# Output projection and second MLP product in seven quarter products instead of eight

## Chip, cores and metric

One core of a Trainium2 chip runs the kernel. The metric is the device time in microseconds. The five engines keep their own instruction queues and run them in order: TensorE (PE, with its weight loads PEld), VectorE (DVE), ScalarE (ACT), GpSimd (POOL) and SyncE (SP), which here only issues DMAs. TensorE writes its sums into PSUM; weights and activations lie in SBUF, and all inputs come from HBM by DMA.

## What is computed

One layer of a hybrid decoder block on 512 tokens of width 1024. Four token mixers are merged under gates (`mixed`), then an output projection, a residual, a second RMSNorm and an MLP follow:

```python
    proj = jnp.einsum('bsnc,ncd->bsnd', ys, w_branch[l])
    gates = jax.nn.sigmoid(jnp.einsum('bsd,de->bse', xn, w_gate[l]) + b_gate[l]).reshape(B, S, N_MIXERS, D)
    mixed = jnp.sum(gates * proj, axis=2)
    x = x + jnp.einsum('bsd,de->bse', mixed, w_out[l])
    hn = _rms(x, norm2_g[l])
    hid = jnp.square(jax.nn.relu(jnp.einsum('bsd,df->bsf', hn, w_mlp1[l])))
    x = x + jnp.einsum('bsf,fd->bsd', hid, w_mlp2[l])
```

`w_out` is 1024 x 1024, `w_mlp1` 1024 x 4096, `w_mlp2` 4096 x 1024, all float32.

## The kernel before

**Products in three matmuls.** Every float32 operand is split into a rounded part and a rest (`split`, L73 to L76): ScalarE casts the source to the type `F32R` (`hi`, L74), VectorE subtracts it from the source (`lo`, L75). `mm3` (L78 to L81) then issues three matmuls, hi x hi, hi x lo and lo x hi, into one PSUM sum. A matmul takes a 128 x 128 stationary operand and streams up to 512 columns.

**Weight stream.** `pieces` is the list of weight pieces in the order of use. `piece` (L91) gives each a `load`, a DMA on SyncE's queue (L102) into one of four `raw` buffers of 128 x 1024 floats, and a `make`, which splits the raw piece into `hi` and `lo`, three buffers each. `take` (L123) returns the next piece, makes two pieces ahead of it and loads two further.

**Order of the work.** The Tile planner (L1065) puts each engine's instructions in order when the kernel is built, from simulated times, the earlier in the program first among those ready. On the chip an engine then runs its list in that order and waits by semaphores.

**Stages.** Projections, attention, gating and convolutions come first; the last of them is `gate_branch` (from L797), where each of eight 128-column blocks `dt` of `MIX` (features on partitions, tokens along the free side) gets its last term, and in the last branch VectorE's sum is at once split into `MH`, `ML`. GpSimd adds the terms of the middle branches (L828). Then:
- *Output projection* (L923 to L944): for each half `q` of the output columns and each of four token tiles `t`, eight k-tiles times three matmuls of 512 columns, 192 in all. L936 adds the sum to the residual `X1`; ScalarE squares it, and for `q == 1` `norm_scale` (L300) and `norm_tr` (L309, eight transposes) make the normed, transposed, split input `HH`, `HL` of the MLP. `tr_task` puts the transposes of one tile between later matmuls.
- *MLP* (L967 to L1019): for each half `fh` of the 32 blocks of hidden features, first the product with `w_mlp1` (24 matmuls of 512 columns a block, `mlp1_part`; relu on ScalarE, square on VectorE L961, split into `hdh`, `hdl`); the very first three blocks run their first 256 tokens before the second 256, which gives the last norms time (L971 to L978). Then `out_mm` (L996) for each half `q` of the output columns: eight pieces of two hidden blocks each, 24 matmuls a piece, 768 over the four passes; L1017 adds to `X1`, and the last passes store the output. The last tile is cut into two halves of 256 columns.

Of the kernel before, what the change touches and what calls it, by code (L numbers as in the profile page):

```python
# [8 lines left out]
F32 = mybir.dt.float32  # L9
# [3 lines left out]
ALU = mybir.AluOpType  # L13
# [14 lines left out]
HPW = 268  # L28

# [8 lines left out]
def block_kernel(ctx: ExitStack, tc: tile.TileContext, x, w_in, w_branch, w_gate, w_out,  # L38
# [7 lines left out]
    big = left.enter_context(tc.tile_pool(name="big", bufs=1))  # L46
    right = ctx.enter_context(ExitStack())
# [43 lines left out]
    def piece(name, srcs, nk, alloc=None):  # L91
# [3 lines left out]
        def load():  # L95
            if st:
                return
            raw = wp.tile([P, 4 * HPW], F32, tag="raw", name=f"raw_{name}", bufs=4)
# [29 lines left out]
    KV0 = big.tile([P, 2, 2, 4 * MW], F32R, tag="mix", name="KV0")  # L128
# [10 lines left out]
    wop = []  # L139
# [20 lines left out]
    for q in range(2):  # L160
        for k in range(4):
            piece(f"wo{q}{k}", [w_out[k * 256 : (k + 1) * 256, q * 512 : (q + 1) * 512]], 2,
                  lambda tag, nm: wop[0].tile([P, 4 * HPW], F32R, tag=tag, name=f"{tag}_{nm}"))
    NH = NF // 2
    for fh in range(2):
        for f in range(fh * NH, (fh + 1) * NH):
            piece(f"m1_{f}", [w_mlp1[:, f * P : (f + 1) * P]], 8)
        for q in range(2):
            for f0 in range(fh * NH, (fh + 1) * NH, 2):
                piece(f"m2_{q}{f0}", [w_mlp2[f0 * P : f0 * P + 256, q * 512 : (q + 1) * 512]], 2)  # L170

# [622 lines left out]
    MIX = big.tile([P, KT, S], F32, tag="mix", name="MIX")  # L794
    MH, ML = [], []

    def gate_branch(i, n, Yf):  # L797
        last = i == 3
        Y = None
        for c4 in range(4):  # L800
# [15 lines left out]
            for j in range(2):  # L816
# [80 lines left out]
    wop.append(att_stack.enter_context(tc.tile_pool(name="wop", bufs=4, side="right", reuse_waits="tile")))  # L897
# [9 lines left out]
    left.close()  # L907
    mp = ctx.enter_context(tc.tile_pool(name="mp", bufs=1, reuse_waits="tile"))
    X1 = mp.tile([P, NT, D], F32, name="X1")
    for t in range(NT):  # L910
        nc.scalar.dma_start(X1[:, t, :], x[t * P : (t + 1) * P, :])
    HH = mp.tile([P, KT, S], F32R, name="HH")
    HL = mp.tile([P, KT, S], F32R, name="HL")
    SS2 = mp.tile([P, NT, 2], F32, name="SS2")
    g2 = mp.tile([P, 2, 512], F32, name="g2")
    nc.scalar.dma_start(g2.rearrange("p h c -> p (h c)"), norm2_g.partition_broadcast(P))
    hss = {}

# [150 lines left out]
```

## Time and profile before

| | |
|---|---|
| median of 3 runs | 832.77 us (832.64 to 833.12) |
| profiled execution, first to last instruction | 831.0 us |
| PE busy | 822.4 us (99%), 4097 matmuls |
| DVE busy | 426.7 us (51%) |
| ACT busy | 299.6 us (36%) |
| POOL busy | 86.1 us (10%) |
| DMA | 81.34 MB, mean 98 GB/s |

An engine's busy time is the union of its instructions' spans. TensorE's matmuls are pipelined: each row shows one as some 0.39 us long, and the step from one start to the next is what it costs. The time between the span and the median, 1.7 us, is start and end of the program outside of the profiled instructions.

### The profile page before, as it was taken

Reading aid. Unit: us, or ns where it says so; the run is one execution under the profiler, and the core shown is the slowest. Engines: PE = TensorE matmul, PEld = TensorE weight load, DVE = VectorE, ACT = ScalarE, POOL = GpSimd, SP = SyncE. Lnnn points to the kernel's source line nnn. Section 1 sums busy time; section 2 is a strip of 40 time slices with the busy share of each in tenths; the row PEclk is TensorE's granted clock in tenths of the full one; section 3 lists DMA queues with packets and bytes.
Section 4 is the critical chain, followed back from the end, with each engine's and each line's share of the span. In section 5 each row is a group of like instructions: output and inputs, shape, how many; then the busy total and the mean of one; then the engine's idle time right before and its main releaser. Section 6 shows DMA issues by size and latency. Waiting matters only on the chain.

```text
span 831.0 us, 10391 instructions
## 1 busy us (share of the span) xinstructions
PE 822.4 (99%) x4097; PEld 674.7 (81%) x4097; DVE 426.7 (51%) x766; ACT 299.6 (36%) x507; POOL 86.1 (10%) x82
## 2 busy tenths in 40 slices
PE   7999999999999999999999999999999999999998
PEld 5989787777787888888888888888888888888887
DVE  5967764346999446734625754442232444442321
ACT  6636533444423325423515344341121334332110
POOL 6011011221443121220000000000000000000000
PEclk9999999999999999999999999999999999999999
DMA  9282222321222232333536032323233233223401
GB/s 307 81 196 60 87 66 79 87 77 52 63 65 89 77 91 87 97 93 91 198 142 175 3 102 80 98 103 101 77 102 102 81 96 102 101 77 102 152 26 51
DMA packets 108979, 81.34 MB, mean 98 GB/s; under 512 B 3873, under 2 KB 96321, under 8 KB 108930
## 3 DMA queue, kind: packets, MB, share of 16 engines
q1 hardware_dynamic: 107666, 76.61, 30.4%
q10 hardware_dynamic: 720, 2.62, 0.9%
q0 software_dynamic: 544, 1.45, 0.6%
q8 instruction: 32, 0.52, 0.3%
q14 instruction: 17, 0.14, 0.0%
HBM read 78.05 MB, written 2.10 MB: 96 GB/s over the span
## 4 chain that ended last, share of the span: by engine, by line
PE 97%; DMA 1%; SPq 1%; ACT 0%; DVE 0%; issue 0%
PE gt L79 7%; PE gt L81 7%; PE h L81 7%; PE h L79 7%; PE h L80 7%; PE gt L80 7%; PE o L79 7%; PE o L80 7%; PE o L81 7%; PE pj L79 2%; PE pj L81 2%; PE wo L80 2%; PE wo L79 2%; PE wo L81 2%; PE pj L80 2%; PE pv L548 2%
## 5 line engine op out<-in xcount | busy, mean ns | idle before, releaser
L75 DVE TENSOR_TENSOR lo_m<-raw_m,hi_m 128x1024 fp32r<-128x1024 f32 x64 | 78.4, 1225 | 176.8 <-ACT hi_m L74 176.8
L74 ACT CAST hi_m<-raw_m 128x1024 fp32r<-128x1024 f32 x64 | 67.1, 1049 | 195.9 <-PE o L81 107.1
L81 PE MATMUL h<-HH,lo_m 128*128 128x512 f32 (+1 forms) x280 | 104.9, 375 | 0.0
L79 PE MATMUL h<-HH,hi_m 128*128 128x512 f32 (+1 forms) x280 | 104.5, 376 | 0.2 <-ACT HH L74 0.2
L80 PE MATMUL h<-HL,hi_m 128*128 128x512 f32 (+1 forms) x280 | 104.5, 374 | 0.0
L79 PE MATMUL gt<-XH,hi_wg 128*128 128x512 f32 x256 | 101.8, 398 | 0.0
L81 PE MATMUL gt<-XH,lo_wg 128*128 128x512 f32 x256 | 101.2, 395 | 0.0
L80 PE MATMUL gt<-XL,hi_wg 128*128 128x512 f32 x256 | 100.7, 393 | 0.0
L79 PE MATMUL o<-hi_m,hdh 128*128 128x512 f32 x240 | 95.0, 396 | 0.0
L80 PE MATMUL o<-lo_m,hdh 128*128 128x512 f32 x240 | 94.9, 395 | 0.0
L81 PE MATMUL o<-hi_m,hdl 128*128 128x512 f32 x240 | 94.3, 394 | 0.0
L75 DVE TENSOR_TENSOR lo_wg<-raw_wg,hi_wg 128x1024 fp32r<-128x1024 f32 x32 | 39.1, 1222 | 61.9 <-ACT hi_wg L74 61.8
L74 ACT CAST hi_wg<-raw_wg 128x1024 fp32r<-128x1024 f32 x32 | 33.5, 1047 | 83.0 <-PE gt L80 57.9
L81 PEld LDWEIGHTS h<-HH,lo_m 128*128 128x128 f32 x280 | 52.7, 188 | 10.4
L80 PEld LDWEIGHTS h<-HL,hi_m 128*128 128x128 f32 x280 | 52.7, 188 | 10.2
L79 PEld LDWEIGHTS h<-HH,hi_m 128*128 128x128 f32 x280 | 52.3, 188 | 10.1 <-ACT HH L74 0.5
L526 POOL TENSOR_SCALAR p<-p,c 128x128 f32<-128x128 f32 (+3 forms) x32 | 42.8, 1347 | 153.8 <-DVE c L524 141.8
L81 PEld LDWEIGHTS gt<-XH,lo_wg 128*128 128x128 f32 x256 | 48.1, 188 | 11.8 <-issue 0.5
L80 PEld LDWEIGHTS gt<-XL,hi_wg 128*128 128x128 f32 x256 | 48.2, 188 | 10.7
L79 PEld LDWEIGHTS gt<-XH,hi_wg 128*128 128x128 f32 x256 | 48.1, 188 | 10.7 <-issue 0.3
L81 PEld LDWEIGHTS o<-hi_m,hdl 128*128 128x128 f32 x240 | 45.0, 188 | 11.0
L79 PEld LDWEIGHTS o<-hi_m,hdh 128*128 128x128 f32 x240 | 45.2, 188 | 10.6
(368 smaller groups left out, 1439.8 us busy)
## 6 DMA issues: line engine op xcount, KB each, us to landing
raw_m<-in_w_mlp_dram SPq DMA_DIRECT2D x64, 512.0 KB, 3.6
raw_wg<-in_w_gate_dram SPq DMA_DIRECT2D x32, 512.0 KB, 3.9
raw_wb<-in_w_branch_dram SPq DMA_DIRECT2D x16, 256.0 KB, 2.6
raw_wo<-in_w_out_dram SPq DMA_DIRECT2D x8, 512.0 KB, 4.2
x<-in_x_dram SPq DMA_DIRECT2D x4, 512.0 KB, 6.6
raw_kv<-in_w_in_dram SPq DMA_DIRECT2D x4, 512.0 KB, 4.7
w<-in_cmp_w_dram SPq DMA_DIRECT2D x4, 512.0 KB, 6.0
X<-in_x_dram ACTq DMA_DIRECT2D x4, 512.0 KB, 6.7
```

The source lines that it names most:

```text
L74: i = nc.scalar.copy(hi, src)
L75: (eng or nc.vector).tensor_tensor(out=lo, in0=src, in1=f32(hi), op=ALU.subtract)
L79: nc.tensor.matmul(dst, l[0], r[0], start=start, stop=False)
L80: nc.tensor.matmul(dst, l[0], r[1], start=False, stop=False)
L81: nc.tensor.matmul(dst, l[1], r[0], start=False, stop=stop)
L526: nc.gpsimd.tensor_scalar_mul(p_[:, b, :w], p_[:, b, :w], c2[:, b : b + 1])
L548: nc.tensor.matmul(dst[i], V[:, k, b, g * HD : (g + 1) * HD], pts[h - 1 + i][:, b, k * P : (k + 1) * P], start=False, stop=b == 1 and k == t)
```

## The change

Both products named are cut into 2 x 2 quarters, C = A B with A the activations (token halves `h` by k halves) and B the weights (k halves by column halves), and computed as Strassen's seven products instead of eight. `PROD` lists for each product which quarters of A and of B it takes with which signs, and to which quarters of C its sum is added. Five of the seven take a sum or difference of two quarters of B, five one of two quarters of A.

- `block_piece` takes the place of `piece` for these weights. One such piece is a quarter's strip of 256 rows and 512 columns. It loads one or two strips (`raw`, four buffers, and `raw2`, three), adds or subtracts two in place on GpSimd, splits the result into `hi`, `lo` as before, forms the sum of two activation strips (128 x 512) on VectorE where one is wanted, and splits that too.
- The output projection takes the products in the order 3, 5, 4, 7, 1, 2, 6 with two pieces each, the MLP's second product takes eight pieces for each: products 3 and 6, whose A lies in the first half of the hidden features, are put between the blocks 16 to 31 of the first MLP product, one piece behind each block (`M2_EARLY`); products 4, 2, 1, 5, 7 follow (`M2_LATE`).
- A piece is 12 matmuls of 512 columns (two token tiles, two k-tiles, three matmuls). `block_add` adds a finished product to one or two quarters of `X1`, 128 x 1024 each, straight from PSUM.
- `MIX` and the hidden activations `HID` stay in float32 until their pieces are made; the splits in `gate_branch` and in `mlp1_done` go. `norm2` runs for the token tiles 0 and 1 behind product 1 and for 2 and 3 behind the last product, each over the whole row.

```diff
+    PROD = {
+        1: (((0, 0, 1), (1, 1, 1)), ((0, 0, 1), (1, 1, 1)), ((0, 0, 1), (1, 1, 1))),
+        2: (((1, 0, 1), (1, 1, 1)), ((0, 0, 1),), ((1, 0, 1), (1, 1, -1))),
+        3: (((0, 0, 1),), ((0, 1, 1), (1, 1, -1)), ((0, 1, 1), (1, 1, 1))),
+        4: (((1, 1, 1),), ((1, 0, 1), (0, 0, -1)), ((0, 0, 1), (1, 0, 1))),
+        5: (((0, 0, 1), (0, 1, 1)), ((1, 1, 1),), ((0, 0, -1), (0, 1, 1))),
+        6: (((1, 0, 1), (0, 0, -1)), ((0, 0, 1), (0, 1, 1)), ((1, 1, 1),)),
+        7: (((0, 1, 1), (1, 1, -1)), ((1, 0, 1), (1, 1, 1)), ((0, 0, 1),)),
+    }
...
+    def block_piece(name, prod, p, B, kh, A):
...
+            for i, (k, n, _) in enumerate(bq):
+                if i == 0:
+                    raw = wp.tile([P, 4 * HPW], F32, tag="raw", name=f"raw_{name}", bufs=RAWS)
+                else:
+                    raw = hcp[0].tile([P, 1024], F32, tag="raw2", name=f"raw2_{name}", bufs=3)
+                rv = raw[:, :1024].rearrange("p (k c) -> p k c", k=2)
+                r0 = (k * kh + 2 * p) * P
+                nc.sync.dma_start(rv, B[r0 : r0 + 256, n * 512 : (n + 1) * 512].rearrange("(k p) c -> p k c", p=P))
...
+        def make():
+            load()
+            raw = st["raw"]
+            if len(bq) == 2:
+                nc.gpsimd.tensor_tensor(out=raw[0], in0=raw[0], in1=raw[1], op=op_of(bq[1][2]))
+            w = [walloc(tag, name)[:, :1024] for tag in ("hi", "lo")]
+            split(raw[0], w[0], w[1])
+            src = [A()[:, k * kh + 2 * p : k * kh + 2 * p + 2, h * 256 : (h + 1) * 256] for h, k, _ in aq]
+            if len(aq) == 2:
+                hs = hcp[0].tile([P, 2, 256], F32, tag="hc", name=f"hc_{name}", bufs=2)
+                nc.vector.tensor_tensor(out=hs, in0=src[0], in1=src[1], op=op_of(aq[1][2]))
+                src[0] = hs
+            a = [hcp[0].tile([P, 2, 256], F32R, tag=f"hc{i}", name=f"hc{i}_{name}", bufs=3) for i in range(2)]
+            split(src[0], a[0], a[1])
...
+    WO_ORDER = (3, 5, 4, 7, 1, 2, 6)
...
+    M2_EARLY, M2_LATE = (3, 6), (4, 2, 1, 5, 7)
+    plan = [("f", f) for f in range(NH)]
+    for i in range(NH):
+        plan += [("f", NH + i), ("s", M2_EARLY[i // NP], i % NP)]
+    plan += [("s", prod, p) for prod in M2_LATE for p in range(NP)]
...
-                if last:
-                    if dt % 2 == 0:
-                        MH.append(t4(f"MH{dt}", [P, 2, S], F32R))
-                        ML.append(t4(f"ML{dt}", [P, 2, S], F32R))
-                    split(mx, MH[-1][:, dt % 2, :], ML[-1][:, dt % 2, :])
...
+    HID = hp.tile([P, NF, S], F32, name="HID")
+    X1 = hp.tile([P, NT, D], F32, name="X1")
     for t in range(NT):
         nc.scalar.dma_start(X1[:, t, :], x[t * P : (t + 1) * P, :])
...
+    HH, HL = XH, XL
...
+    def block_part(acc, p, np_):
+        w, a = take(1, 2)[0]
+        for t in range(2):
+            block_mm(acc[:, t, :], w, a, t, p == 0, p == np_ - 1)
+
+    def block_add(prod, acc):
+        for h, n, sign in PROD[prod][2]:
+            xv = X1[:, 2 * h : 2 * h + 2, n * 512 : (n + 1) * 512]
+            nc.vector.tensor_tensor(out=xv, in0=xv, in1=acc, op=op_of(sign))
...
+    for prod in WO_ORDER:
+        acc = ps2(f"wo_{prod}")
+        for p in range(2):
+            block_part(acc, p, 2)
+            tick()
+        block_add(prod, acc)
+        if prod == 1:
+            norm2(0)
+            norm2(1)
+    norm2(2)
+    norm2(3)
...
     def mlp1_done(f, acc):
-        r = hp.tile([P, S], F32, tag="rl", name=f"rl_{f}", bufs=2)
+        r = HID[:, f, :]
         nc.scalar.activation(out=r, in_=acc, func=AF.Relu)
         nc.vector.tensor_tensor(out=r, in0=r, in1=r, op=ALU.mult)
-        hh = hp.tile([P, S], F32R, tag="hdh", name=f"hdh_{f}")
-        hl = hp.tile([P, S], F32R, tag="hdl", name=f"hdl_{f}")
-        split(r, hh, hl)
-        hid[f] = (hh, hl)
...
+    for it in plan[3:]:
...
+        block_part(acc, p, NP)
+        if p == NP - 1:
+            finished(prod, acc)
```

The last product (7) is written out apart: its second token tile is cut into two halves of 256 columns, as the last tile was before.

## Rows read from the trace of the kernel before

**Rows 1.** The page, part 1: busy us, share of the span, instructions.
```profile
PE 822.4 (99%) x4097; PEld 674.7 (81%) x4097; DVE 426.7 (51%) x766; ACT 299.6 (36%) x507; POOL 86.1 (10%) x82
```

**Rows 2.** The page, part 4: the chain that ended last, by engine.
```profile
PE 97%; DMA 1%; SPq 1%; ACT 0%; DVE 0%; issue 0%
```

**Rows 3.** Windows, projection, MLP pass: PE, PEld, DVE, ACT, POOL busy; clock; DMA.
```profile
421.50:468.20 46.70, 46.46 (x210) 37.67 (x208) 25.14 (x50) 16.99 (x31) 0.00 (x0) 1.00 0.44 136
559.60:643.50 83.90, 83.90 (x361) 67.61 (x360) 22.93 (x22) 16.82 (x17) 0.00 (x0) 1.00 0.29 94
```

**Rows 4.** Timeline, output projection, PE: start us, duration us, instruction; thirteen starts.
```profile
457.20 0.39 PE L80 MATMUL wo<-lo_wo,MH 128*128 128x512 f32 x1
...
459.99 0.39 PE L80 MATMUL wo<-lo_wo,MH 128*128 128x512 f32 x1
```

**Rows 5.** Lines by form, DVE and ACT: busy us, mean ns, idle before.
```profile
L75 DVE TENSOR_TENSOR lo_m<-raw_m,hi_m 128x1024 fp32r<-128x1024 f32 x64 | 78.4, 1225 | 176.8 <-ACT hi_m L74 176.8
L961 DVE TENSOR_TENSOR rl<-rl 128x512 f32<-128x512 f32 x32 | 21.9, 684 | 0.0
...
L74 ACT CAST hi_m<-raw_m 128x1024 fp32r<-128x1024 f32 x64 | 67.1, 1049 | 195.9 <-PE o L81 107.1 <-PE h L80 61.2 <-PE o_11h L81 22.8
L74 ACT CAST hdh<-rl 128x512 fp32r<-128x512 f32 x32 | 19.9, 621 | 42.0 <-DVE rl L961 42.0
```

**Rows 6.** Timeline around two of GpSimd's sums: start us, duration us.
```profile
337.67 1.22 DVE L75 TENSOR_TENSOR lo_wg<-raw_wg,hi_wg 128x1024 fp32r<-128x1024 f32 x1
337.83 2.21 POOL L828 TENSOR_TENSOR MIX<-MIX,g 128x512 f32<-128x512 f32 x1 [10.72 <-DVE g L827]
...
338.80 1.78 DVE L658 SCALAR_TENSOR_TENSOR cv<-csq,cv 128x512 f32<-128x512 f32 x1
...
341.11 0.68 DVE L75 TENSOR_TENSOR YC<-cv,YC 128x512 fp32r<-128x512 f32 x1
341.27 1.67 POOL L828 TENSOR_TENSOR MIX<-MIX,g 128x512 f32<-128x512 f32 x1 [1.23 <-DVE g L827]
341.71 1.78 DVE L75 TENSOR_TENSOR lo_wb<-raw_wb,hi_wb 128x512 fp32r<-128x512 f32 x1
```

**Rows 7.** Timeline, two further sums of GpSimd and VectorE beside them.
```profile
294.57 2.99 POOL L828 TENSOR_TENSOR MIX<-MIX,g 128x512 f32<-128x512 f32 x2 [11.45 <-DVE g L827]
...
294.67 0.69 DVE L827 SCALAR_TENSOR_TENSOR g<-g,pj 128x512 f32<-128x512 f32 x1 [0.17 <-PE pj L81]
```

**Rows 8.** Timeline near the start: GpSimd's widest sums.
```profile
13.37 1.27 DVE L75 TENSOR_TENSOR lo_q<-raw_q,hi_q 128x1072 fp32r<-128x1072 f32 x1
...
13.98 5.28 POOL L75 TENSOR_TENSOR KV<-raw_kv,KV 128x1024 fp32r<-128x1024 f32 x2 [3.64 <-ACT KV L74]
```

**Rows 9.** Windows near the start, where the DMA engines are busiest; columns as in rows 3.
```profile
10.00:15.00 5.00, 4.81 (x21) 4.16 (x20) 4.50 (x10) 3.70 (x5) 1.36 (x2) 1.00 1.11 363
15.00:20.00 5.00, 4.92 (x40) 4.71 (x39) 2.01 (x6) 3.30 (x7) 4.26 (x2) 1.00 1.11 351
```

**Rows 10.** Timeline, the last token tile's norm, from its residual add on.
```profile
467.21 0.68 DVE L936 TENSOR_TENSOR X<-X,wo 128x512 f32<-128x512 f32 x1
468.14 1.29 DVE L75 TENSOR_TENSOR HL<-tr_n,HH 128x512 fp32r<-128x512 f32 x2 [0.24 <-ACT HH L74]
469.53 0.15 DVE L230 TENSOR_SCALAR rsv_n<-ss 128x1 f32<-128x1 f32 x1
471.77 1.41 DVE L305 SCALAR_TENSOR_TENSOR hs<-X,r_n,g 128x512 f32<-128x512 f32 x2
```

**Rows 11.** Timeline, PE, matmuls of 268 columns, early and later.
```profile
12.45 0.43 PE L79 MATMUL q<-hi_q,XH 128*128 128x268 f32 x1
12.68 0.43 PE L80 MATMUL q<-lo_q,XH 128*128 128x268 f32 x1
...
15.68 0.29 PE L79 MATMUL q<-hi_q,XH 128*128 128x268 f32 x1
15.81 0.29 PE L80 MATMUL q<-lo_q,XH 128*128 128x268 f32 x1
```

More of the change, by code (lines that the diff above doesn't have):

```diff
@@ L947, in block_kernel, with block_mm @@
-    right.close()
-    hp = right.enter_context(tc.tile_pool(name="hp", bufs=16, side="right", reuse_waits="tile"))
-    hid = {}
+    HH, HL = XH, XL
+    g2 = HID[:, NF - 2 : NF, :]
+    nc.scalar.dma_start(g2, norm2_g.rearrange("o (h c) -> o h c", h=2).partition_broadcast(P))
+    def block_mm(dst, w, a, t, first, last, c0=0, n=512):
+        for j in range(2):
+            sl = slice(t * P, (t + 1) * P)
+            mm3(dst, (a[0][:, j, sl], a[1][:, j, sl]), (w[0][:, j, c0 : c0 + n], w[1][:, j, c0 : c0 + n]),
+                first and j == 0, last and j == 1)
@@ new lines, in block_part, with norm2 @@
+    def block_part(acc, p, np_):
[6 more added lines that the diff above has]
+            nc.vector.tensor_tensor(out=xv, in0=xv, in1=acc, op=op_of(sign))
+    def norm2(t):
+        hs = HID[:, 2 * t + 16 : 2 * t + 18, :].rearrange("p a b -> p (a b)")
+        ss = const.tile([P, 1], F32, tag="ss", name=f"ss2_{t}", bufs=2)
+        nc.scalar.activation(out=hs, in_=X1[:, t, :], func=AF.Square, accum_out=ss)
+        norm_scale(X1[:, t, :], hs, g2, ss, t, "n2")
+        norm_tr(hs, t, "n2", HH, HL, [ps(f"tr_n2{t}{h}") for h in range(2)])
@@ L951, in mlp1_part @@
+    for prod in WO_ORDER:
+        acc = ps2(f"wo_{prod}")
+        for p in range(2):
+            block_part(acc, p, 2)
[6 more added lines that the diff above has]
+    norm2(3)
     def mlp1_part(acc, w, a, b):
@@ new lines, in block_kernel, with finished @@
+    w = take(3, 0)
+    accs = [ps(f"h_{j}") for j in range(3)]
+    for a, b in ((0, 256), (256, 512)):
+        for j in range(3):
+            mlp1_part(accs[j], w[j], a, b)
+    for j in range(3):
+        mlp1_done(j, accs[j])
+    def finished(prod, acc):
+        block_add(prod, acc)
+        for h, n in {2: ((1, 0),), 1: ((1, 1),), 5: ((0, 1),)}.get(prod, ()):
+            for t in range(2 * h, 2 * h + 2):
+                cs = slice(n * 512, (n + 1) * 512)
+                nc.sync.dma_start(out[t * P : (t + 1) * P, cs], X1[:, t, cs])
@@ new lines, in block_kernel @@
+    acc = None
+    for it in plan[3:]:
+        if it[0] == "f":
+            f = it[1]
+            w, = take()
+            h = ps(f"h_{f}")
+            mlp1_part(h, w, 0, 512)
+            mlp1_done(f, h)
+            continue
+        _, prod, p = it
+        if prod == M2_LATE[-1]:
+            break
+        if p == 0:
+            acc = ps2(f"o_{prod}")
+        block_part(acc, p, NP)
+        if p == NP - 1:
+            finished(prod, acc)
+    a0 = ps("o_l0")
+    a1 = [ps(f"o_l1{i}") for i in range(2)]
@@ new lines, in block_kernel @@
+    parts = [(0, a0, 0, 512), (1, a1[0][:, :256], 0, 256), (1, a1[1][:, :256], 256, 256)]
+    for p in range(NP - 2):
+        w, a = take(1, 2)[0]
+        for t, d, c0, n in parts:
+            block_mm(d, w, a, t, p == 0, False, c0, n)
+    wa = take(2, 1)
+    for t, d, c0, n in parts:
+        for i in range(2):
+            block_mm(d, wa[i][0], wa[i][1], t, False, i == 1, c0, n)
+        cs = slice(c0, c0 + n)
+        nc.vector.tensor_tensor(out=X1[:, t, cs], in0=X1[:, t, cs], in1=d, op=ALU.add)
+        nc.sync.dma_start(out[t * P : (t + 1) * P, cs], X1[:, t, cs])
```

128 lines of the change are left out of this document (28 added, 100 removed).

## Prediction

> **What bounds the kernel now.** I read the page's busy times first: TensorE is busy 99% of the span, VectorE half of it, GpSimd a tenth [rows 1]. The chain that ended last says the same: PE 97% [rows 2]. An average says nothing of one stage, so the two stages that change come next. In the output projection and in an MLP output pass TensorE is busy without a break; VectorE is busy 25.1 of 46.7 us in the first and 22.9 of 83.9 us in the second, GpSimd not at all, and the DMA engines move 136 and 94 GB/s [rows 3]. The reader is to see two things there: fewer matmuls mean less time one for one, as long as the others keep up; and there is much room on the others, but it is room in a stage where GpSimd does nothing.
>
> The price of a matmul is the step between starts, not the length of a row: from 457.20 to 459.99 us lie twelve steps of 512 columns, 0.2325 us each [rows 4].
>
> **What the change removes.** Output projection 192 to 7 x 2 x 12 = 168 matmuls, second MLP product 768 to 7 x 8 x 12 = 672: 120 fewer, 120 x 0.2325 = 27.9 us, all on the path. The counts are fixed in the code, so that the change does not do this is no case. A piece of 12 matmuls now lasts 2.79 us of TensorE; within that time its operands must be made. The splits of `MIX` and of the hidden features go, but they lay beside matmuls.
>
> **What it adds, per piece.** VectorE: `lo` of 128 x 1024, start to start 1.13 us (337.67 to 338.80); `lo` of the activations, 128 x 512, 0.60 us (341.11 to 341.71); where A is a sum, one more of 512, 0.60 us [rows 6]. That is 1.73 or 2.33 us, under 2.79. ScalarE: casts of 1.05 and 0.62 us [rows 5], 1.67 us: hidden. GpSimd: where B is a sum (products 1, 3, 4, 6, 7) one addition of 128 x 1024, and here lies the matter.
>
> Rows 6 and 7 show GpSimd's additions and VectorE side by side. A VectorE instruction that reads two SBUF operands and a GpSimd addition do not overlap. At 337.67 VectorE starts first (until 338.89); the GpSimd addition issued at 337.83 ends at 340.04, 1.15 us after VectorE; the VectorE instruction issued at 338.80 ends at 340.58, 0.54 us after GpSimd, and shows 1.78 us for work that takes 0.68. The same again at 341.11: ends at 341.79, 342.94, 343.49. Ten of the sixteen GpSimd additions of that line and eight VectorE instructions beside them are lengthened in this way. Where VectorE reads one operand from PSUM, as at 294.67, it keeps its 0.69 us beside a running addition [rows 7]. So the two engines take turns on something that two SBUF operands need. The turn of a 128 x 1024 addition: `lo_q` ends at 14.64, two additions end at 19.26 [rows 8]: 2.31 us each.
>
> Every `lo` and every activation sum of the change reads two SBUF operands; `block_add` reads PSUM and escapes. The turns of a piece add up:
> - A single, B summed (products 3, 4): 2.31 + 1.13 + 0.60 = 4.04 us
> - both summed (1, 6, 7): 2.31 + 1.13 + 0.60 + 0.60 = 4.64 us
> - A summed, B single (2, 5): 2.33 us, so TensorE's 2.79 us counts
>
> The Trainium skill (SBUF — State Buffer, section Who interferes with whom) gives the rule: a VectorE instruction with two SBUF inputs and a GpSimd instruction that reads SBUF exclude each other, and the second waits for the whole first. By whole instructions (1.225 and 0.69 us [rows 5, 7] for 1.13 and 0.60) the two dearer kinds of piece would be 4.23 and 4.92 us and the forecast below 853 us; the steps in rows 6 are a little shorter, and I go by them.
>
> **The late MLP products** (4, 2, 1, 5, 7, eight pieces each): 8 x 4.04 + 16 x 4.64 + 16 x 2.79 = 151.1 us against 40 x 2.79 = 111.6 of TensorE. Work done ahead shortens it: at the start two pieces are made and four `raw` buffers can hold finished sums, 2 x 4.04 + 4 x 2.31 = 17.3 us. The last piece's matmuls come behind it, 2.8. So 136.6 us, 25.0 over TensorE's own. Bounds: VectorE's turn may be as short as the 0.54 us behind GpSimd (1.08 for 1024), and products 2 and 5 may lend their slack to later sums: 24 x 2.31 + 40 x 1.08 + 72 x 0.54 = 137.5, less 17.3, plus 2.8: +11. Above: VectorE runs in order, an activation sum is followed by a cast on ScalarE (0.62) before its `lo`, and whatever stands behind that `lo` waits too: 32 x 0.62 = 20 us, if nothing fits between, and the eight `block_add` (1.13 each) may fall beside no addition, 9 us; of these 29, products 2 and 5 swallow 7: +47. The middle terms are nearest to rows 6; I keep +25.0.
>
> **The early MLP products** (3, 6) stand behind blocks of the first product: a pair has 36 matmuls, 8.4 us, against turns of 4.64 + 1.13 + 0.60 (L961 reads two SBUF operands, too) = 6.4 us. Hidden; if the pair's order broke that, it would cost at most the 16 x 1.85 us by which a 4.64 piece alone exceeds its own 2.79. Nothing taken.
>
> **The output projection:** 4 x 4.04 + 6 x 4.64 + 4 x 2.79 = 55.2 us; the norms of token tiles 0 and 1 now fall among its last products: per tile 1.41 (L305) + 1.29 (`HL`) + six small ones of 0.15 [rows 10], 7.2 for both. Ahead of it, beside the last gates, two pieces and two sums are done (product 5 has no sum and takes two buffers): 12.7 us less. With the last piece's 2.8: 52.5 against 14 x 2.79 = 39.1: +13.4. Bounds: +5 with the shorter turns and the norms beside sums; +34 if the twelve `block_add` (13.6) and ten waits of 0.62 lie in the open. `X1` is loaded on ScalarE's queue as before, now into other memory; the casts of the next pieces stand behind its four issues and the first `block_add` comes one product in; a late landing is inside that upper bound.
>
> **The last norms.** Tiles 2 and 3 are both normed behind product 6. From the last residual add to the end of L305 one tile took 467.21 to 473.18, 6.0 us [rows 10]; now the add and the squaring are twice as wide (+0.5, +0.4), the second tile is behind the first (+1.4), and transposes, a cast and two `HL` follow (about 2.4): 10.7 us. The cover is the same as before, 72 half matmuls of 0.116 us: 8.4. I take 2.5 us; 0 if the planner finds other work, 6 if the splits of the next weights stand in between.
>
> **DMA.** A piece with two strips moves 1.05 MB; near the start the queues delivered 351 and 363 GB/s [rows 9]: 2.9 to 3.0 us, less than 4.04. It costs nothing while the turns are the bound; without them, some 34 pieces x 0.2 = 7 us.
>
> **Sum.** Against the profiled execution: 831.0 - 27.9 + 25.0 + 13.4 + 2.5 = 844.0 us of span; with the 1.7 us between span and median, 845.7. Forecast 846.
>
> **Rivals.**
> - *The room is enough* (faster): if additions and subtractions hardly met, VectorE alone would need 2.2 us a piece plus 0.23 for the adds, and all is hidden: 832.8 - 27.9 + 2.5 = 807, with the DMA's 7 us 814. It decides if a GpSimd turn is below (111.6 + 17.3 - 2.8 - 40 x 1.13 - 72 x 0.60) / 24 = 1.6 us. For it: VectorE is idle most of rows 3. Against it: 2.31 us in rows 8, and no exception among the sums beside two-operand work. Chance 0.10.
> - *In-order waits add up* (slower still): the upper bounds of both stages, 832.8 - 27.9 + 47 + 34 + 2.5 = 888; likelier most of it than all, 870 to 888. For it: ScalarE and VectorE alternate within a piece, as the idle time behind `hi_m` shows [rows 5]. Against: the planner may put the next piece's `lo` between. Chance 0.15.
> - *TensorE's clock.* Now TensorE waits within every dear piece. At 12.45 us, when it had run only scattered work before, 268 columns took a step of 0.23 us, at 15.68, after some 5 us of nearly closed work, 0.13 [rows 9, 11]: the levels of 1.2 and 2.4 GHz. At the lower level a piece takes 12 x 0.23 x 512 / 268 = 5.3 us, more than its turns: 24 late pieces +60, ten of the projection +25, in all 892. No row shows whether a share of 60% busy lowers it. Chance 0.08.
> - *The forecast*, 820 to 870 around 846: 0.67. Some 0.06 of it lie below 831.
>
> **How the numbers follow.** Faster: 0.10 + 0.06 = 0.16. Within 0.2%, which is about what a measurement of this kernel can tell from no change (831.1 to 834.4): 0.03. Slower: 0.81. The range leaves out the first rival and the ends of the second and third: 820 to 884.
>
> **What would show it.** Right: in the late stretch TensorE idle about 18%, waiting for VectorE's `lo`; GpSimd additions of 2.4 us when alone and up to 3.6 beside VectorE; VectorE's `lo` well above 1.23 us on average for products 1, 4, 7 and near it for 2 and 5; the stretches of 2 and 5 at TensorE's pace. Wrong: TensorE closed through products 1 and 7 (first rival); `lo` at 1.23 us and SyncE or the landing of `raw2` last (DMA); steps of 0.44 us between matmuls (clock); GpSimd idle and VectorE waiting for ScalarE (second rival).

## The result, and the profile after

The changed kernel takes 865.45 us (median of 4 runs, 864.04 to 866.71) against 832.7 of the kernel before: ratio 1.039, 95% interval 1.0376 to 1.0405. The profiled execution spans 862.3 us. The direction was forecast and the time lies in the range, but the loss is 32.8 us where 13 were expected.

The page of the changed kernel, part 1 and the line by engine of part 4, which answer to [rows 1, 2]:

```profile
PE 810.5 (94%) x3977; PEld 657.2 (76%) x3977; DVE 601.6 (70%) x873; ACT 342.5 (40%) x559; POOL 225.2 (26%) x132
PE 78%; DVE 11%; issue 6%; DMA 2%; ACT 1%; POOL 1%; SPq 1%; ACTq 0%; DVEq 0%; POOLq 0%
```

120 matmuls fewer, exactly, but TensorE's share of the chain has gone from 97% to 78%. Windows of the changed kernel, columns as in [rows 3]; the four stretches are the projection's matmuls, from the last of them to the first hidden product, the first MLP product with the early pieces (products 3 and 6), and the late pieces (products 4, 2, 1, 5, 7):

```profile
421.40:480.10 58.70, 45.24 (x168) 33.36 (x167) 54.82 (x63) 24.08 (x32) 22.37 (x8) 0.91 0.74 240
480.10:493.40 13.30, 6.27 (x33) 4.93 (x32) 12.31 (x28) 6.92 (x14) 0.00 (x0) 0.74 0.30 87
493.40:713.30 219.90, 219.90 (x1022) 181.91 (x1022) 123.89 (x110) 74.00 (x97) 49.11 (x19) 1.00 0.49 149
713.30:862.30 149.00, 123.78 (x541) 97.37 (x540) 141.65 (x120) 61.73 (x78) 60.66 (x22) 0.96 0.66 211
```

TensorE is closed (busy without a break) in the third stretch, where the pieces of products 3 and 6 stand among other matmuls, and open in the other three; there VectorE is closed, or nearly. Before, the projection's matmuls lay between 421.5 and 466.7, the first hidden product began at 468.2, and the MLP took 362.9 us. Now the projection's matmuls take 58.7 us (45.2 before), the way to the first hidden product 13.3 (1.5 before), the MLP 368.9.

Lines by form, changed kernel, from 712 us to the end (form of [rows 5]):

```profile
L77 DVE TENSOR_TENSOR lo_m<-raw_m,hi_m 128x1024 fp32r<-128x1024 f32 x39 | 62.9, 1612 | 2.8 <-ACT hi_m L76 2.8
L77 DVE TENSOR_TENSOR hc_m<-hc_m,hc_m 128x512 fp32r<-128x512 f32 x32 | 29.9, 948 | 0.2 <-ACT hc_m L76 0.2
L207 DVE TENSOR_TENSOR hc_m<-HID 128x512 f32<-128x512 f32 x30 | 28.8, 978 | 0.1
L985 DVE TENSOR_TENSOR X<-X,o 128x1024 f32<-128x1024 f32 x9 | 10.6, 1212 | 0.0
...
L201 POOL TENSOR_TENSOR raw_m<-raw_m,raw_m 128x1024 f32<-128x1024 f32 x22 | 63.1, 2878 | 75.4 <-DMA raw_m<-in_w_mlp_dram 38.0 <-DVE hc_m L77 27.1 <-DVE hc_m L207 6.0
```

`hc` names the activation strips of a piece, their sums and their splits. The three groups that read two SBUF operands have grown (1.612 for 1.225 us, 0.95 and 0.98 for 0.69); L985, which reads PSUM, keeps 1.21. The timeline of the same kernel, in product 1, shows single meetings as [rows 6] did (start us, duration us):

```profile
773.62 2.34 DVE L985 TENSOR_TENSOR X<-X,o 128x1024 f32<-128x1024 f32 x2
774.77 2.37 POOL L201 TENSOR_TENSOR raw_m<-raw_m,raw_m 128x1024 f32<-128x1024 f32 x1 [2.76 <-issue]
...
777.62 1.21 DVE L77 TENSOR_TENSOR lo_m<-raw_m,hi_m 128x1024 fp32r<-128x1024 f32 x1
777.85 3.22 POOL L201 TENSOR_TENSOR raw_m<-raw_m,raw_m 128x1024 f32<-128x1024 f32 x1 [0.72 <-DVE hc_m L77]
778.75 2.88 DVE L77 TENSOR_TENSOR hc_m<-hc_m,hc_m 128x512 fp32r<-128x512 f32 x1
...
783.54 2.71 POOL L201 TENSOR_TENSOR raw_m<-raw_m,raw_m 128x1024 f32<-128x1024 f32 x1 [2.46 <-DMA raw_m<-in_w_mlp_dram]
783.88 3.44 DVE L77 TENSOR_TENSOR lo_m<-raw_m,hi_m 128x1024 fp32r<-128x1024 f32 x1
```

At 777.85 GpSimd ends 2.24 us after VectorE's `lo_m`, and VectorE's next one 0.56 us after GpSimd. A `lo_m` issued into a sum lasts 3.44 us. Of the two additions to `X1` at 773.62 the second runs beside the sum at 774.77, and both together take 2.34.

### The profile page after: what moved, and what is told of

Read it like the earlier page. It is cut to its first block, busy times and chain, and to the rows that moved or that the text cites. A ratio compares the mean times of both kernels' runs of the same rounds, so it can differ in the third digit from the quotient of the medians.

```text
span 862.3 us, 10726 instructions
## 1 busy us (share of the span) xinstructions
PE 810.5 (94%) x3977; PEld 657.2 (76%) x3977; DVE 601.6 (70%) x873; ACT 342.5 (40%) x559; POOL 225.2 (26%) x132
## 3 DMA queue, kind: packets, MB, share of 16 engines
q0 software_dynamic: 544, 1.45, 0.6%
## 4 chain that ended last, share of the span: by engine, by line
PE 78%; DVE 11%; issue 6%; DMA 2%; ACT 1%; POOL 1%; SPq 1%; ACTq 0%; DVEq 0%; POOLq 0%
PE gt L81 7%; PE gt L83 7%; PE h L81 7%; PE h L83 7%; PE h L82 7%; PE gt L82 7%; PE o L82 3%; PE o L83 3%; DVE lo_m L77 3%; PE o L81 3%; DVE hc_m L77 3%; DVE hc_m L207 2%; PE pj L81 2%; PE pj L83 2%; PE pj L82 2%
## 5 line engine op out<-in xcount | busy, mean ns | idle before, releaser
L77 DVE TENSOR_TENSOR lo_m<-raw_m,hi_m 128x1024 fp32r<-128x1024 f32 x88 | 140.3, 1595 | 96.2 <-ACT hi_m L76 96.2
L201 POOL TENSOR_TENSOR raw_m<-raw_m,raw_m 128x1024 f32<-128x1024 f32 x40 | 109.8, 2750 | 269.6 <-DMA raw_m<-in_w_mlp_dram 173.6
L81 PE MATMUL h<-XH,hi_m 128*128 128x512 f32 (+1 forms) x280 | 105.2, 376 | 0.0
L83 PE MATMUL h<-XH,lo_m 128*128 128x512 f32 (+1 forms) x280 | 105.0, 375 | 0.0
L82 PE MATMUL h<-XL,hi_m 128*128 128x512 f32 (+1 forms) x280 | 104.5, 373 | 0.0
L82 PE MATMUL o<-lo_m,hc_m 128*128 128x512 f32 x192 | 77.3, 402 | 13.2 <-DVE lo_m L77 13.1
L83 PE MATMUL o<-hi_m,hc_m 128*128 128x512 f32 x192 | 76.2, 397 | 0.1
L81 PE MATMUL o<-hi_m,hc_m 128*128 128x512 f32 x192 | 76.2, 397 | 0.0
L83 PEld LDWEIGHTS h<-XH,lo_m 128*128 128x128 f32 x280 | 52.7, 188 | 10.4
L82 PEld LDWEIGHTS h<-XL,hi_m 128*128 128x128 f32 x280 | 52.7, 188 | 10.2
L81 PEld LDWEIGHTS h<-XH,hi_m 128*128 128x128 f32 x280 | 52.6, 188 | 9.7
```

The source lines that it names most:

```text
L77: (eng or nc.vector).tensor_tensor(out=lo, in0=src, in1=f32(hi), op=ALU.subtract)
L81: nc.tensor.matmul(dst, l[0], r[0], start=start, stop=False)
L82: nc.tensor.matmul(dst, l[0], r[1], start=False, stop=False)
L83: nc.tensor.matmul(dst, l[1], r[0], start=False, stop=stop)
L201: nc.gpsimd.tensor_tensor(out=raw[0], in0=raw[0], in1=raw[1], op=op_of(bq[1][2]))
```

## Experiments: do the turns carry the loss?

**Sums left out.** `e1_no_sums`: the change without GpSimd's additions; both strips are still loaded, the second is not used.

```diff
-            if len(bq) == 2:
-                nc.gpsimd.tensor_tensor(out=raw[0], in0=raw[0], in1=raw[1], op=op_of(bq[1][2]))
```

> The changed kernel with GpSimd's additions of weight strips left out (both strips are still loaded; the first one alone is split, so five of the seven products are of other weights). Theory (the turns between GpSimd's additions and VectorE's instructions with two SBUF operands hold up the pieces): VectorE alone needs 45.6 + 43.2 + 10.2 = 99 us for the 40 late pieces and their adds, under TensorE's 111.6, so the last stretch (from the first matmul of product 4) falls from 149 us to 115 to 122, the projection from 72 us to 55 to 62: 865 to 815 to 832. Rival DMA (twice the strips to load): the loads are all there, so it stays above 850. Rival in-order waits between ScalarE and VectorE: those are all there too, so it stays above 850.

Measured: 821.46 us, ratio 0.9862 (0.9842 to 0.9881). Windows of its projection, of the way to the first hidden product, and of its late products:

```profile
421.90:468.00 46.10, 40.93 (x168) 32.26 (x167) 43.98 (x62) 23.89 (x32) 0.00 (x0) 0.96 0.65 212
468.00:481.20 13.20, 6.18 (x34) 4.82 (x33) 12.21 (x28) 6.81 (x14) 0.00 (x0) 0.74 0.33 96
701.10:818.90 117.80, 114.10 (x541) 94.59 (x539) 100.59 (x120) 61.35 (x78) 0.00 (x0) 1.00 0.57 175
```

With the same loads 44 us go: 31.2 from the late products, 12.6 from the projection, nothing from the 13 us behind it. The same 120 VectorE instructions of the late stretch show 100.59 us here and 141.65 with the sums. Neither the bytes moved nor the casts and splits alone carry this loss, the sums do. This run doesn't part their turns from two other waits that go with them, a piece's wait for its second strip to land and for GpSimd's result; and the 13.2 us are another matter.

**Sums on VectorE.** `e2_sums_dve`:

```diff
-                nc.gpsimd.tensor_tensor(out=raw[0], in0=raw[0], in1=raw[1], op=op_of(bq[1][2]))
+                nc.vector.tensor_tensor(out=raw[0], in0=raw[0], in1=raw[1], op=op_of(bq[1][2]))
```

> The changed kernel with the additions of weight strips on VectorE instead of GpSimd. Theory of turns: an addition costs VectorE 1.14 us instead of a turn of 2.2, so 24 late ones give back 25 us of the queue's time, 10 in the projection 10; with TensorE's own 111.6 us as a floor: last stretch 149 to some 132, projection 72 to some 66, in all 838 to 850. Rival in-order waits (VectorE's queue is simply too long): 50 more instructions of 1.2 us on VectorE make it slower, 870 or more.

Measured: 856.37 us, ratio 1.0278 (1.0263 to 1.0293): faster than with GpSimd, but by 9 us only, between the theory's range and the rival's. Its VectorE, late products, lines by form:

```profile
L201 DVE TENSOR_TENSOR raw_m<-raw_m,raw_m 128x1024 f32<-128x1024 f32 x21 | 25.7, 1225 | 12.2 <-DMA raw_m<-in_w_mlp_dram 10.4 <-issue 1.7
```

A sum costs 1.2 us there, but it now waits in VectorE's queue for its strips, 12.2 us, and what stands behind it waits too. The late products still took 142.4 us, without a single turn: what a sum costs is its work and its strips' landing as well, not the turn alone.

**Half of the change, each way.** `e5_mlp_only` has the projection and norms of before and the changed MLP.

```diff
-    WO_ORDER = (3, 5, 4, 7, 1, 2, 6)
-    for prod in WO_ORDER:
-        for p in range(2):
-            block_piece(f"wo{prod}{p}", prod, p, w_out, 4, lambda: MIX)
+    for q in range(2):
+        for k in range(4):
+            piece(f"wo{q}{k}", [w_out[k * 256 : (k + 1) * 256, q * 512 : (q + 1) * 512]], 2,
...
```

> Only the MLP part of the change: output projection and its norms as before, second MLP product in seven products with the sums on GpSimd as in the changed kernel. Theory (most of the miss lies in the projection with its norms, the MLP is dearer by what the changed kernel's trace shows there, 368.9 against 362.9 us): 468.2 + 368.9 + 1.7 = 839 us, 836 to 842. Rival (the late stretch was lengthened by what the projection leaves behind, a lower clock or late transfers): the late stretch falls below 145 us and the time to 835 or less. Rival of the prediction's own terms (an MLP of 362.9 + 2.7): 835.

Measured: 841.54 us, ratio 1.0102 (1.0083 to 1.0120); late products 148.8 us, as in the whole change (149.0). The two halves of the loss are independent: some 9 us in the MLP, 24 in the projection.

## Experiments: the projection and what follows it

**Norm step left out.** `e13_no_norm_step`: `norm2` is only its transposes of `X1`.

```diff
-        hs = HID[:, 2 * t + 16 : 2 * t + 18, :].rearrange("p a b -> p (a b)")
-        ss = const.tile([P, 1], F32, tag="ss", name=f"ss2_{t}", bufs=2)
-        nc.scalar.activation(out=hs, in_=X1[:, t, :], func=AF.Square, accum_out=ss)
-        norm_scale(X1[:, t, :], hs, g2, ss, t, "n2")
-        norm_tr(hs, t, "n2", HH, HL, [ps(f"tr_n2{t}{h}") for h in range(2)])
+        norm_tr(X1[:, t, :], t, "n2", HH, HL, [ps(f"tr_n2{t}{h}") for h in range(2)])
```

> The second norm's squares, scale steps and weight product are left out: the transposes take X1 as it is; the rest is the changed kernel. Theory (of the 13 us from the last projection matmul to the first hidden product some 9 are the norms' chain, squares, small VectorE steps and products of both tile pairs one behind the other in VectorE's and ScalarE's queues): first hidden product 4 to 6 us behind the last projection matmul, 854 to 858 us in all. Rival (that stretch is set by the additions and by VectorE's backlog from the projection, whatever the norms do): 10 us or more behind it, 862 to 866.

Measured: 855.87 us, ratio 1.0284 (1.0262 to 1.0307). TensorE's timeline between the last projection matmul and the first hidden product:

```profile
482.64 0.40 PE L83 MATMUL wo<-hi_wo,hc_wo 128*128 128x512 f32 x1
484.35 1.53 PE L376 MATMUL tr_n<-ident,X 128*128 128x128 f32 x12 [1.31 <-DVE X L983]
485.64 0.36 PE L81 MATMUL h<-XH,hi_m 128*128 128x256 f32 x1
```

3.0 us in place of 13.3. (The projection's matmuls took 61.0 us for 58.7 and the late products 147.8 for 149.0, so 9.6 of the 10.3 us arrive at the end.)

**Cover for the last norms.** The changed kernel issues all transposes ahead of the first half matmuls of the hidden product; before, those of the last tiles came between the halves. `e3_norms_later` puts tiles 2 and 3 there again:

```diff
-    norm2(2)
-    norm2(3)
...
     for a, b in ((0, 256), (256, 512)):
+        if a:
+            norm2(2)
+            norm2(3)
```

> The changed kernel with the norms of token tiles 2 and 3 written behind the first half matmuls of the first three MLP blocks, as in the kernel before; in the built program the half matmuls now stand ahead of the transposes of tiles 2 and 3. Theory (in the changed kernel these 8.4 us of cover are lost, as TensorE's list has the transposes first and TensorE stands still for 7 us before them): 5 to 8 us less, 857 to 860. Rival (the norms are late because VectorE is behind with everything, so the half matmuls wait too): within 2 us of 865.

Measured: 868.95 us, ratio 1.0431 (1.0416 to 1.0447): a miss. The first hidden product came 3.5 us earlier, but the transposes of tiles 2 and 3 waited in turn for the one PSUM bank that the three open hidden blocks left free, from 500.8 to 507.5 us. `e3b_norms_later_ps2` gives them the two-bank area:

```diff
-        norm_tr(hs, t, "n2", HH, HL, [ps(f"tr_n2{t}{h}") for h in range(2)])
+        norm_tr(hs, t, "n2", HH, HL, [ps(f"tr_n2{t}{h}") for h in range(2)] if t < 2 else None)
```

> As in the kernel with the norms of tiles 2 and 3 behind the first half matmuls, but their transposes go to the PSUM area of two banks, which is free there, and not to the single banks that the first three hidden blocks hold. Theory (the last norms cost 13 us in the open, and the former kernel gave its gain back because the transposes waited in turn for one bank): first hidden product at about 490 us, the early stretch back at 220 to 223 us, 859 to 862 us in all. Rival (the chain of squares, scales and transposes is as long as the 8.4 us of cover and more): 865 to 869.

Measured: 865.27 us, ratio 1.0389 (1.0374 to 1.0405): the rival's value. First hidden product at 488.5, 4.9 us earlier; TensorE's timeline from there shows where they went:

```profile
490.13 0.41 PE L82 MATMUL h<-XL,hi_m 128*128 128x256 f32 x1
490.34 0.41 PE L83 MATMUL h<-XH,lo_m 128*128 128x256 f32 x1
...
499.60 0.28 PE L83 MATMUL h<-XH,lo_m 128*128 128x256 f32 x1
499.71 1.04 PE L376 MATMUL tr_n<-ident,HID 128*128 128x128 f32 x8
501.71 1.25 PE L376 MATMUL tr_n<-ident,HID 128*128 128x128 f32 x8 [0.96 <-DVE XL L77]
503.05 0.62 PE L81 MATMUL h<-XH,hi_m 128*128 128x256 f32 x3
```

Until 494 the half matmuls went at a step of 0.21 us, later 0.117: the granted clock was 0.5, and that part of the cover cost nearly double. The normed tiles 2 and 3 were ready at 493.5, but their transposes stand behind the last of the 72 half matmuls, and the second eight wait for the splits of the first: 3.3 us from 499.71 to the next product.

**What holds the norms of tiles 0 and 1.** Product 1 completes their rows at 466.4 us, yet they are normed at 482.6. The chain of the changed kernel (start us, duration us) passes from a load to the norm's steps:

```profile
469.30 7.40 DMA raw_m<-in_w_mlp_dram
...
476.80 1.05 ACT hi_m L76
...
477.88 1.23 DVE lo_m L77
479.10 0.07 DVE r_n L293
...
479.95 0.64 DVE HID L366
...
482.60 1.14 DVE X L985
```

`raw_m` is a weight piece of the first MLP product, made two pieces ahead. Its cast and split stand in ScalarE's and VectorE's queues ahead of steps of the norm that have nothing to do with it. The price is small: VectorE stood idle for 1.45 us ahead of the split and took 1.23 for it; from 467.6 to 476.4 us it had been busy, for the most part with the last products' operands and additions. The last projection matmul was done at 480.5 us and its addition, the line at 482.60, began some 2 us later, behind the norm steps. From there to the first hidden product it is 10.9 us, and the prediction had 10.7 for this chain. `e17_w1_behind_norms` makes these pieces behind the norms in the program:

```diff
-            block_part(acc, p, 2)
+            block_part(acc, p, 2, 1 - p if prod == 6 else 2)
```

> The changed kernel, but the first two weight pieces of the first MLP product are made behind the norms in the program, not ahead of product 6's end; their loads stay. In the changed kernel the norm steps of tiles 0 and 1 (479.0 to 482.6 us) stand in VectorE's queue behind a split of such a piece, which waited for its strip until 476.7. Theory (this in-order wait is a part of the 13 us behind the last projection product): tiles 0 and 1 are normed by about 477, first hidden product 3 to 6 us earlier, 860 to 863 us; less if the late splits of the weights then hold the first hidden product. Rival (the norms are held by the projection's own work in VectorE's queue): tiles 0 and 1 no earlier than 480, 865 to 867.

Measured: 865.52 us, ratio 1.0391 (1.0374 to 1.0408), and no test of the theory: the planner put the split in the same place again, ahead of the norm steps. It speaks in another way. Timeline of VectorE, the split and the step behind it:

```profile
480.07 1.23 DVE L77 TENSOR_TENSOR lo_m<-raw_m,hi_m 128x1024 fp32r<-128x1024 f32 x1 [2.58 <-ACT hi_m L76]
481.21 0.16 DVE L293 RECIPROCAL r_n<-rsu_n 128x1 f32<-128x1 f32 x1
```

The split came 2.2 us later than in the changed kernel, though the last projection matmul came 0.5 us earlier (479.6), and the first hidden product came 2.2 us later (495.6). What the norms would do without it wasn't brought about.

**PSUM and the load of `X1`.** TensorE stood still for 4.87 us before 441.4 us, for an area of PSUM that VectorE had not yet emptied; the additions that empty it stand behind a split that met a sum of GpSimd. Timeline of the changed kernel:

```profile
436.14 2.90 POOL L201 TENSOR_TENSOR raw_wo<-raw_wo,raw_wo 128x1024 f32<-128x1024 f32 x1 [5.05 <-DVE lo_wo L77]
436.76 3.36 DVE L77 TENSOR_TENSOR lo_wo<-raw_wo,hi_wo 128x1024 fp32r<-128x1024 f32 x1
440.05 3.47 DVE L985 TENSOR_TENSOR X<-X,wo 128x1024 f32<-128x1024 f32 x3
441.40 0.77 PE L81 MATMUL wo<-hi_wo,hc_wo 128*128 128x512 f32 x1 [4.87 <-DVE X L985]
```

`e4_more_psum` lets the products take three areas in turn (the two two-bank areas and, for every second product, a pair of single banks):

```diff
+        two = i % 2 == 1 and prod != 6
+        if two:
+            accs = [ps(f"wo_{prod}{t}") for t in range(2)]
...
```

> The changed kernel with the projection's products taking turns between three PSUM areas instead of two (every second product sums into two single banks). Theory (the stop of some 5 us ahead of the third product is a wait for the first product's block_add, which stands in VectorE's queue behind a subtraction that waits for GpSimd): 3 to 6 us less, 859 to 862. Rival (the third product's own operands are late by as much): within 2 us of 865.

Measured: 870.56 us, ratio 1.0453 (1.0436 to 1.0471): a miss; the projection with its norms took 79.1 us, and TensorE's longest waits were 9.8 us for a ScalarE cast and 8.6 for the norm; why it got slower wasn't followed up. Another suspect is the load of `X1`, for which the first additions wait. `e14_no_residual` leaves out the load of `X1`, and the first addition to each quarter becomes a copy:

```diff
-    for t in range(NT):
-        nc.scalar.dma_start(X1[:, t, :], x[t * P : (t + 1) * P, :])
...
+            if (h, n) in begun:
+                nc.vector.tensor_tensor(out=xv, in0=xv, in1=acc, op=op_of(sign))
+            else:
+                nc.vector.tensor_copy(out=xv, in_=acc)
+                begun.add((h, n))
```

> The residual is left out: X1 is not loaded, and the first addition to each of its four quarters becomes a copy out of PSUM; everything else is the changed kernel. Theory (besides the turns, the late landing of X1 at 432 us held VectorE's first additions and through the two PSUM areas TensorE, some 5 us before 441 us): last projection matmul 3 to 5 us earlier, 860 to 862 us. Rival (VectorE's queue is closed there anyhow, the wait only moves): last projection matmul within 1 us of 480, 864 to 866.

Measured: 863.50 us, ratio 1.0360 (1.0341 to 1.0379); the projection's matmuls end 57.9 us after their start instead of 58.7, at 479.6 us, which is the rival's sign, though the time lies between the two ranges. The wait of 4.87 us is gone, and one of 4.13 for a split stands further on: it moves.

**The additions to `X1`.** `e8_first_adds` keeps one of the two for each product:

```diff
-        for h, n, sign in PROD[prod][2]:
+        for h, n, sign in PROD[prod][2][:1]:
```

> Of each finished product only the first addition to a quarter of X1 is left in, the second one is left out: five additions of 128 x 1024 less in the projection and five less in the MLP, one of these behind an early product. Theory (the additions read PSUM and so don't exclude GpSimd, but they lie in VectorE's queue, which is closed in both stages, and GpSimd does nothing beside most of them): each is worth its 1.13 us, nine of them 10 us, 853 to 858. Rival (the prediction's premise, that they lie beside GpSimd's turns and cost nothing): 863 to 865.

Measured: 863.79 us, ratio 1.0365 (1.0346 to 1.0384): the rival's value. The projection's matmuls gave 2.7 us (56.0), but the way to the first hidden product took 1.2 more and the late products 1.9 more. `e16_no_adds_no_norm` goes on from the kernel without the norm step and leaves out all twelve of the projection:

```diff
             tick()
-        block_add(prod, acc)
```

> As the kernel without the norm step, and the twelve additions to X1 in the projection are left out as well, so that nothing waits for them either. Its projection took 61.0 us from the first to the last matmul with them. Theory (the additions read PSUM and so need no turn, but they take VectorE's queue in the open and hold the two PSUM areas): 6 to 13 us less, 48 to 55 us from first to last, 843 to 850 us in all. Rival (the prediction's premise: they lie beside GpSimd's sums and cost nothing; the turns alone set the stage): 59 to 61 us, 853 to 856 in all.

Measured: 845.73 us, ratio 1.0159 (1.0141 to 1.0178). Windows of the projection's matmuls, first without the norm step, then without the additions too:

```profile
421.60:482.70 61.10, 47.89 (x189) 36.45 (x187) 57.45 (x55) 22.85 (x30) 24.06 (x8) 0.86 0.71 225
```

```profile
421.50:474.70 53.20, 45.62 (x201) 35.66 (x200) 49.82 (x47) 24.19 (x33) 19.34 (x8) 0.97 0.73 243
```

7.9 us for twelve additions, or 0.66 us each, as the theory had it. This is an upper bound of what they cost in VectorE's queue alone: without them the areas of PSUM are free at once, the transposes of `X1` wait for nothing, and the granted clock is 0.97 instead of 0.86. These were not separated.

## Experiments: a place where the products pay

`e10_half_hidden` keeps the projection of before and uses the seven products only for the hidden features 0 to 15: its 28 pieces are spread between the blocks 16 to 31 of the first product. Features 16 to 31 follow as plain quarter products, without sums. The sums of weights are on VectorE.

```diff
+    GROUPS = [(0, 16, True), (16, 32, False)]
...
+    for f0, f1, strassen in GROUPS:
+        n, m = f1 - f0, len(late)
+        for i in range(n):
+            plan.append(("f", f0 + i))
+            plan += late[m * i // n : m * (i + 1) // n]
+        late = blocks(f0, f1, strassen)
```

> Output projection as before. Hidden features 0 to 15 by the seven products, 28 pieces spread between the blocks 16 to 31 of the first MLP product (36 to 48 matmuls, 8.4 to 11.2 us, for each block and its pieces); features 16 to 31 by plain quarter products behind them; sums of weights on VectorE. 48 matmuls fewer than before, 11.2 us. Theory (a seven-product piece is free where TensorE has 8 us or more of its own work for it: VectorE needs at most 1.75 x 4.7 us a block and has it to itself): 832.8 - 11.2 = 821.6, with quarter products at 2.79 us a piece against 1.73 of VectorE closed, 820 to 825. Rival (the seven products cost more in waits than they save wherever they stand): 830 or more.

Measured: 821.67 us, ratio 0.9864 (0.9850 to 0.9879). `e12_half_hidden_gpsimd` is the same with the sums on GpSimd:

```diff
-                nc.vector.tensor_tensor(out=raw[0], in0=raw[0], in1=raw[1], op=op_of(bq[1][2]))
+                nc.gpsimd.tensor_tensor(out=raw[0], in0=raw[0], in1=raw[1], op=op_of(bq[1][2]))
```

> As the kernel with half of the features by seven products, but the sums of weights on GpSimd as in the change. By turns a block and its 1.75 pieces need 9.3 us of VectorE and GpSimd together (first product 1.13 + 0.60, pieces 1.75 x 2.2, sums 1.25 x 2.31, additions 0.8) against 10.5 of TensorE. Theory (turns cost their sum and no more, and are free below TensorE's time): 821 to 824 us, like the kernel with the sums on VectorE. Rival (each meeting of the two engines also delays what stands behind, so that the turns cost more than their sum): 828 or more.

Measured: 821.83 us, ratio 0.9866 (0.9850 to 0.9883). Windows of 120 us within the mixed stretch, first sums on VectorE, then on GpSimd, and from the latter GpSimd's line:

```profile
600.00:720.00 120.00, 120.00 (x519) 97.13 (x518) 89.49 (x99) 48.71 (x63) 0.00 (x0) 1.00 0.57 179
```

```profile
600.00:720.00 120.00, 120.00 (x519) 97.12 (x518) 95.01 (x88) 48.95 (x63) 33.33 (x12) 1.00 0.58 184
...
L204 POOL TENSOR_TENSOR raw_m<-raw_m,raw_m 128x1024 f32<-128x1024 f32 x12 | 33.3, 2789 | 85.1 <-DMA raw_m<-in_w_mlp_dram 63.7 <-DVE hc_m L77 9.1 <-issue 6.8
```

The turns are there (2.79 us a sum), TensorE is closed all the same. `e11_three_quarters_hidden` makes four groups of eight blocks, three of them by seven products, with the sums on VectorE:

```diff
-    GROUPS = [(0, 16, True), (16, 32, False)]
+    GROUPS = [(0, 8, True), (8, 16, True), (16, 24, True), (24, 32, False)]
```

> As the kernel with half of the features by seven products, but in four groups of eight blocks: the second MLP product of the first, second and third group runs in seven products (14 pieces) between the blocks of the group that follows, that of the last group in plain quarter products. 72 matmuls fewer than before, 16.7 us. Theory (VectorE has 8.6 us to do in a block and its pieces, TensorE 10.5, so all is hidden): 816 to 820 us. Rival (twelve additions to X1 in each group instead of twelve for two groups, 0.8 us a block more, close VectorE): 822 or more.

Measured: 816.10 us, ratio 0.9799 (0.9784 to 0.9814): the fastest kernel here, 16.8 us below before for 72 matmuls x 0.2325 = 16.7.

## Why the prediction was right in direction and short in size

The span was forecast at 844.0 and came at 862.3, 18.3 us more. By its terms:

1. **Matmuls saved:** right. 120 fewer; the kernels that hide everything else get 0.2325 us for each.
2. **The turns:** right as a mechanism, by single meetings and by the 41 us by which the late VectorE instructions are longer with the sums than without; TensorE is idle for 17% of that stretch, where 18 was the sign. By the prediction's steps the late products take 136.6 us, by whole instructions (8 x 4.23 + 16 x 4.92 + 16 x 2.79, less 17.3, plus 2.8) 142.7; from the first late matmul (716.1) to the end of the last (858.7) it was 142.6. The Trainium skill (SBUF — State Buffer, section Who interferes with whom) states that the second instruction is blocked for the whole of the first; the meetings shown agree: a sum ends 2.24 us behind the split that it met, and a split of 512 ends 0.56 us behind the sum. That the whole stretch agrees as well is in part luck (point 4).
3. **Early products hidden:** right, 219.90 of 219.90 us closed.
4. **Late products, 136.6 us:** 6.0 too short, 142.6 measured, and not by one part. Windows of the changed kernel, products 4, 2, 1 and 5, columns as before:

```profile
716.10:742.60 26.50, 23.15 (x97) 17.74 (x96) 26.43 (x20) 12.65 (x16) 12.45 (x5) 1.00 0.83 268
742.60:766.70 24.10, 22.45 (x97) 17.96 (x96) 24.09 (x22) 11.00 (x14) 8.88 (x3) 1.00 0.68 212
766.70:800.10 33.40, 25.50 (x97) 18.45 (x96) 33.40 (x31) 14.33 (x18) 13.72 (x5) 0.95 0.75 242
800.10:823.30 23.20, 22.67 (x97) 17.77 (x95) 23.20 (x23) 11.31 (x14) 7.53 (x3) 1.00 0.72 228
```

Products 2 and 5 run near TensorE's 22.3 us, as forecast, and three sums each begin in them, a slack that the term left unused. Products 1 and 7 took 33.4 and 35.4 us where eight turns of 4.64 make 37.1; product 4 took 26.5 where the work done ahead was to leave TensorE's 22.3. So the misses go both ways. What makes up the 6.0 wasn't settled by a run; leaving out four additions there won nothing. For the MLP as a whole 3.3 remain: before, it was 1536 x 0.2325 = 357.1 us of matmuls and 5.8 of others, now 960 x 0.2325 = 223.2, 142.6 and 3.1 of others, as the 16 transposes of the last token tiles no longer lie in it (point 6).
5. **The projection's matmuls:** failed. 45.2 - 5.6 + 13.4 = 53.0 was expected, 58.7 measured, 5.7 more. The failing step is "`block_add` reads PSUM and escapes". It escapes the turn, as its 1.21 us shows, but not VectorE's queue, which is the bound of the stage. To be free it would have had to lie beside a sum of GpSimd, and of the twelve only the three at 440 us did. The prediction had this as an upper bound (13.6 us for twelve) and took nothing; the run without them gave 7.9, an upper bound as well. The miss of this term is larger than 5.7: of the 7.2 us allowed for the norms only some 1 us fell into this stretch (their products begin at 479.9), so that the rest is some 12 us short. A second step is short by the trace, though no run tested it: of the four sums taken as done ahead two were done, and the third began when the matmuls had run for 7 us; two sums are 4.6 us. Timeline of the changed kernel, the second and the third:

```profile
419.95 2.41 POOL L201 TENSOR_TENSOR raw_wo<-raw_wo,raw_wo 128x1024 f32<-128x1024 f32 x1 [8.63 <-issue]
428.70 2.38 POOL L201 TENSOR_TENSOR raw_wo<-raw_wo,raw_wo 128x1024 f32<-128x1024 f32 x1 [6.34 <-DVE hc_wo L207]
```

6. **The last norms, 2.5 us:** failed, the largest miss. 13.3 us lie between the last projection matmul and the first hidden product, where 1.5 + 2.5 were expected: 9.3 more. The length of the chain was right (10.9 us from the last addition, 10.7 forecast); its cover was not. "The cover is the same as before" overlooked that all transposes now stand ahead of the half matmuls, so that none of the 8.4 us lies beside the chain. And the norms of tiles 0 and 1, taken as done within the projection, end at 482.6 and hold the last addition by some 2 us; what stood ahead of them was VectorE's work for the last products and a split that waited for a load. The prediction named "the splits of the next weights" as its bound and gave that 6 us. The run without the norm step shows the size (10.3 us less in the stretch, 9.6 in all). In the two runs that move the cover back the first hidden product comes 3.5 and 4.9 us earlier, and nothing of it is left at the end: by their timelines a slow clock and a second row of waits take it.

5.7 + 9.3 + 3.3 = 18.3, the whole difference. Of the rivals, *in-order waits add up* was half right: waits in VectorE's queue made part of the miss, but with the additions and around the norms, and no run shows the rival's own, those between ScalarE and VectorE within a piece. *TensorE's clock* came true in five short stretches, in part where VectorE is closed anyway (last section). *The room is enough* fell in the two stages where TensorE has 2.79 us a piece, and holds where it has 8 us or more: with the sums left on GpSimd, the same pieces among blocks of the first product cost nothing.

## What to carry to other kernels

A cheaper product on TensorE is worth its matmuls only where the engine that makes its operands has at least as much room per piece; put such pieces among matmuls that need less preparation, rather than one behind the other. An operation that escapes a conflict still takes its place in its engine's queue: when that queue is the bound, count it at up to its full price until a trace shows the cover. When the end of a stage moves, ask of each step there what stands ahead of it on its engine and which load that waits for.

## Not expected of the hardware

The prediction had no row for TensorE at 60% busy. Windows of the changed kernel in the late products show one, columns as above:

```profile
773.00:780.00 7.00, 4.16 (x17) 3.13 (x18) 7.00 (x7) 2.62 (x3) 4.52 (x2) 1.00 0.69 231
780.20:783.40 3.20, 3.12 (x8) 1.92 (x6) 3.20 (x4) 0.62 (x1) 0.88 (x1) 0.50 0.90 258
783.60:790.00 6.40, 5.42 (x22) 3.90 (x23) 6.40 (x5) 2.62 (x3) 4.57 (x2) 1.00 0.81 232
```

After 7 us with 4.16 busy the granted clock fell to 0.50 (1.2 GHz), and the step of 512 columns from 0.23 to 0.43 us; 3.2 us of nearly closed work later it was back. It falls for some microseconds and returns, five times in this kernel before its end; the forecast's rival of a low clock throughout (892 us) did not happen. VectorE is closed in all three windows, so here no cost of the clock shows. In the last piece of the projection one does:

```profile
476.30:479.70 3.40, 3.29 (x8) 2.64 (x9) 1.96 (x11) 1.15 (x2) 0.00 (x0) 0.51 1.13 293
```

TensorE is all but closed at the low level and VectorE is not; seven steps take 2.9 us where 0.2325 each make 1.6. This is 1.3 us of the projection's 58.7.
